# Links of a compressed-attention branch moved in among the query, key and value products, and conv taps and gate products moved within the attention

## The chip, the cores and the metric

One core of a Trainium2 chip runs the whole program. The time is that of the device, in microseconds (us), from the start to the end of one execution; lower is better. Three executions of the kernel before gave 759.12, 759.73 and 758.73 us, median 759.12 us.

The engines are named as in the profile: PE (TensorE, the matrix engine; PEld is its loading of the stationary operand), DVE (VectorE), ACT (ScalarE), POOL (GpSimd) and SP (SyncE, which issues the DMAs here). SBUF is the on-chip memory, PSUM the eight banks of 512 f32 per partition into which PE writes.

## The reference, cut to what matters

One layer with 512 positions, 1024 features and 8 heads in 2 groups. Left out here are the norms, the conv branch's last steps and the whole MLP behind it, which the change does not touch.

```
proj = rms_norm(x) @ w_in      # q | k_c v_c k_s v_s k_w v_w | g_nsa | u_conv | g_merge
# compressed branch: overlapping blocks of 32 positions, stride 16, become one key and one value each
def compress(kv, pe, w1, w2):
    blk = kv[:, idx] + pe                       # 31 blocks x (32*64) per group
    return gelu(blk @ w1) @ w2
kc, vc = compress(k_c, pe_k, ck1, ck2), compress(v_c, pe_v, cv1, cv2)
p_c = softmax(q . kc * scale - slope * dist)    # masked; the "cmp scores"
o_c = p_c @ vc
o_s, o_w = attention over the selected blocks and over the window (k_s, v_s and k_w, v_w)
o = sigmoid(g)[0] * o_c + sigmoid(g)[1] * o_s + sigmoid(g)[2] * o_w
# conv branch
z = a * sigmoid(gate); z = causal_dwconv(z, width 31); y_conv = silu(layer_norm(z)) @ w_conv_br
x = x + (sigmoid(g_a) * (o @ w_attn_br) + sigmoid(g_b) * y_conv) @ w_out
x = x + conv_ffn(rms_norm(x)); out = rms_norm(x)
```

With 8 blocks of 64 positions and a top-16 choice, all blocks are selected, and the window is as long as the sequence, so that the kernel does two dense causal attentions for each head beside the compressed one.

## The kernel before, in words

**Precision.** Every f32 operand of a large product is split into a high part and a low part (a cast on ACT, a subtraction on DVE or POOL), and a product is three PE products: high x high, high x low, low x high. `gemm` (L275) yields after every PE product, so that a caller can take one at a time; with K=8 it is 24 products of 512 columns.

**Weights.** The class `Weights` (L33) brings units of 1 MB by SP's queue (two `raw` buffers), and each unit's two halves are split into `wh` (ACT, L91) and `wl` (POOL, L93), four buffers of each.

**Order.** The code is traced in a program order, and a scheduler then orders each engine's queue: it takes, at each point of its own modelled time, the earliest instruction in program order that it holds to be ready. Each engine then runs its queue in that order and waits where an input is not there. Program order is therefore a priority, not the order itself.

**PSUM.** `psum(tag, name)` (L267) takes a bank of a tag: `mm`, `s` and `t` have two banks each, `o` and `y` one each. `psum_any` (L270) goes round `mm`, `s`, `t`. A bank is free again when the last reader of its former tile has finished.

**SBUF.** `big` (L132) takes one of 27 slots of 4 KB per partition.

**The stage of the change (L485 to L583).** First come the conv branch's input (four chunks `zy`), then `ck`, `cv` (the compressed branch's keys and values, L523), the four query products q0 to q3 (L530), the two key products k0, k1 (L547) and the value products (L566: 96 products of 280 columns into four banks, of which the loop over `kq` does a quarter each time). The compressed branch is a chain of links for k and one for v: `blocks` (DVE, ACT), `hidden` (16 PE products, then ACT L392 and DVE L393), `gelu` (two PE products `hTk`/`hTv` at L398, then ACT L400), then for k `comp_k` (ACT L408, DVE L409, two PE products `kc` at L412 and L413, then ACT and DVE), and for v `comp_v` (ACT, DVE, four PE products `vc` at L430, then ACT L433, DVE L434 and others). In the kernel before, `hidden("k")` stands behind q1, `hidden("v")` behind q3, `gelu("k")` behind k0, `gelu("v")` behind k1, and `comp_k` and `comp_v` after both, ahead of the value products. `cmp_scores` (L440) does 16 PE products of 64 columns (`sc`) for one half of the positions, then a softmax on DVE, POOL and ACT.

**The conv taps.** Each of the four chunks has one ACT instruction (`first`, L493) and 30 DVE instructions (`tap`, L499), 31 items, all appended to the list `pend`. `bg(n)` (L294) traces the next n of them. `bg(BG0)` traces 80 ahead of the cmp scores; the remaining 44 are traced in the attention, each behind the latest row reduction (`last["ttr"]`, DVE L707), and none earlier on DVE than that. From `conv_sum` on (steps `CONV_AT`) the conv branch's LayerNorm follows, up to `cB` (L671, L672).

**The attention (L784 to L812).** 16 steps (8 heads x 2 kinds), cut into 133 pieces (`atoms`): `qk` (PE products `s` at L721 and L727, DVE L707, ACT exp L709), `soft` (DVE L735, then POOL or DVE L739), `ptr` (PE transposes `t` L749, ACT L752, DVE L753) and `pv` (PE products `o` L763 and L769, ACT L775, DVE L777). Between the pieces `fill(n)` traces n of 480 filler products: the 16 merge-gate products (`g`, 384 PE products, bank tag `mm`, each evicted by ACT L593), then the 96 products `cb` of the conv branch, which need `cB`. Before the `cb` products stand four sigmoids on ACT (L601), placed behind the latest exp.

The number of fillers after a piece is this line, and that of taps the one above it:

```
        bg(-(-len(pend) // max(1, nbg - n)))
        fill(int(left[0] / (len(atoms) - n + 0) * 1.1 + 0.5))
```

Behind the attention come the branch projections (`ab`, L837), the merge, the output projection `o0acc` and the MLP (`ua`, `uv`, `d0acc`), which the change leaves as they are.

Of the kernel before, what the change touches and what calls it, by code (L numbers as in the profile page):

```python
# [115 lines left out]
def hybrid_block_kernel(ctx: ExitStack, tc: tile.TileContext, x, norm1_g, w_in, cmp_pe_k, cmp_pe_v,  # L116
# [150 lines left out]
    def psum(tag, name, pl=None):  # L267
        return psB.tile([P, S], F32, tag=tag, name=name, bufs=NB[tag])

    def psum_any(name):  # L270
        tag = ("mm", "s", "t")[cyc[0] % 3]
        cyc[0] += 1
        return psum(tag, name)
# [20 lines left out]
    def bg(n):  # L294
        for _ in range(min(n, len(pend))):
            pend.pop(0)()
# [88 lines left out]
    def hidden(kv):  # L385
        ws = W.get(f"w1{kv}", 0, lead=1) + W.get(f"w1{kv}", 1)
        ps = psum_any(f"hid{kv}")
        for j in range(16):
            mm(ps[:, :256], lhsT=BL[kv][j // 8][:, j % 8].rearrange("p a b -> p (a b)"),
               rhs=ws[j // 4][:, j % 4].rearrange("p a b -> p (a b)"), start=(j == 0), stop=(j == 15))  # L390
        t1 = big(f"ht{kv}", (P, 2, P))
        act.copy(t1[:, 0], ps[:, P : 2 * P])  # L392
        vec.tensor_tensor(t1[:, 1], ps[:, 0:P], t1[:, 0], op=ALU.add)  # L393
        HT[kv] = t1

    def gelu(kv):
        p2 = psum_any(f"hT{kv}")
        mm(p2[:, :64], lhsT=HT[kv][:, 1], rhs=J, start=True, stop=True)  # L398
        ge = cf[:, 4 + "kv".index(kv)]
        act.activation(ge, p2[:, :64], AF.Gelu_apprx_tanh)  # L400
        GEL[kv] = ge

    kc = bp.tile([P, 2, 2, 32], F32R, tag="kc", name="kc")
    vc = bp.tile([P, 2, 2, 64], F32R, tag="vc", name="vc")

    def comp_k():
        gl = cr[:, 6:8]
        act.copy(gl[:, 0], GEL["k"])  # L408
        vec.tensor_tensor(gl[:, 1], GEL["k"], gl[:, 0].bitcast(F32), op=ALU.subtract)  # L409
        ps = psum_any("kc")  # L410
        rhs = gl.rearrange("p a b -> p (a b)")
        mm(ps[:, :P], lhsT=w2kH, rhs=rhs, start=True, stop=False)  # L412
        mm(ps[:, :P], lhsT=w2kL, rhs=rhs, start=False, stop=True)  # L413
        t1, t2 = cf[:, 6], cf[:, 7]
        act.copy(t1, ps[:, 64:128])
        vec.tensor_tensor(t2, ps[:, 0:64], t1, op=ALU.add)
        t2v = t2.rearrange("p (g n) -> p g n", g=2)
        act.copy(kc[:, :, 0], t2v)
        vec.tensor_tensor(kc[:, :, 1], t2v, kc[:, :, 0].bitcast(F32), op=ALU.subtract)

    def comp_v():
        gr = big("gr", (P, 2, 2, 4, 32), F32R)
        src = GEL["v"].rearrange("p (g n) -> p g n", g=2).unsqueeze(2).broadcast_to([P, 2, 4, 32])
        act.copy(gr[:, 0], src)
        vec.tensor_tensor(gr[:, 1], src, gr[:, 0].bitcast(F32), op=ALU.subtract)
        for g in range(2):
            ps = psum_any(f"vc{g}")
            rhs = w2vHL.rearrange("p a b -> p (a b)")
            for part in range(2):
                mm(ps[:, :P], lhsT=gr[:, part, g].rearrange("p a b -> p (a b)"), rhs=rhs,  # L430
                   start=(part == 0), stop=(part == 1))
            t1, t2 = cf[:, 8 + 2 * g], cf[:, 9 + 2 * g]
            act.copy(t1, ps[:, 64:128])  # L433
            vec.tensor_tensor(t2, ps[:, 0:64], t1, op=ALU.add)  # L434
            act.copy(vc[:, g, 0], t2)
            vec.tensor_tensor(vc[:, g, 1], t2, vc[:, g, 0].bitcast(F32), op=ALU.subtract)
# [3 lines left out]
    def cmp_scores(ib):  # L440
        pc = big(f"pc{ib}", (P, 2, 8, 32))
        st = bp.tile([P, 3, 16], F32, tag="cst", name=f"cst{ib}", bufs=2)
        pcf = pc.rearrange("p i h n -> p (i h) n")
        for ii in range(2):
            i = 2 * ib + ii
            ps = psum_any(f"sc{i}")
            pv = ps.rearrange("p (h a n) -> p h a n", h=8, a=2)
            for h in range(NH):
                mm(pv[:, h].rearrange("p a n -> p (a n)"), lhsT=QS[h // 2][:, h % 2, i * P : (i + 1) * P],
                   rhs=kc[:, h // 4].rearrange("p a n -> p (a n)"), start=True, stop=True)  # L450
            vec.tensor_tensor(pc[:, ii], pv[:, :, 1], ndc[:, i].unsqueeze(1).broadcast_to([P, 8, 32]), op=ALU.add)
            vec.tensor_tensor(pc[:, ii], pv[:, :, 0], pc[:, ii], op=ALU.add)
        vec.tensor_reduce(st[:, 0], pcf, axis=AX.X, op=ALU.max)
        vec.tensor_tensor(pcf, pcf, st[:, 0].unsqueeze(2).broadcast_to([P, 16, 32]), op=ALU.subtract)
        pool.tensor_tensor(pc, pc, sl.unsqueeze(1).unsqueeze(3).broadcast_to([P, 2, 8, 32]), op=ALU.mult)
        act.activation(pc, pc, AF.Exp)
        vec.tensor_reduce(st[:, 1], pcf, axis=AX.X, op=ALU.add)
        vec.reciprocal(st[:, 2], st[:, 1])
        gv = gate[:, 2 * ib : 2 * ib + 2].rearrange("p i (h b) -> p i h b", b=3)[:, :, :, 0]
        s2 = st[:, 2].rearrange("p (i h) -> p i h", i=2)  # L460
        vec.tensor_tensor(s2, s2, gv, op=ALU.mult)
        pool.tensor_tensor(pcf, pcf, st[:, 2].unsqueeze(2).broadcast_to([P, 16, 32]), op=ALU.mult)
        PC.append(pc)
# [59 lines left out]
    for i, kv in enumerate("kv"):  # L523
        ps = psum_any(f"c{kv}")
# [5 lines left out]
    for u in range(2):  # L530
        for i in range(2):
            c = 2 * u + i
            ps = psum_any(f"q{c}")
            run(gemm(ps, W.get(f"q{u}", i), h1))
            qs = big(f"qs{c}", dt=F32R)
            for e in range(2):
                a, b = slice(64 * e, 64 * e + 64), slice(64 - 64 * e, 128 - 64 * e)
                act.activation(qs[a, e], ps[a], AF.Copy, scale=QSC[2 * c + e])
                vec.scalar_tensor_tensor(qs[b, e], ps[a], QSC[2 * c + e], qs[a, e].bitcast(F32),
                                         op0=ALU.mult, op1=ALU.subtract)  # L540
            QS.append(qs)
            if c == 1:
                hidden("k")
            elif c == 3:
                hidden("v")
    KK = {}
    for b in range(2):  # L547
        ps = psum_any(f"k{b}")
        run(gemm(ps, W.get("k", b), h1))
        kf = big(f"kf{b}")[:, 0]  # L550
        act.copy(kf, ps)
        for g in range(2):
            kk = big(f"kk{b}{g}", dt=F32R)
            a, o_ = slice(64 * g, 64 * g + 64), slice(64 - 64 * g, 128 - 64 * g)
            for d in (a, o_):
                act.copy(kk[d, 0], kf[a])
            vec.tensor_tensor(kk[a, 1], kf[a], kk[a, 0].bitcast(F32), op=ALU.subtract)
            pool.tensor_tensor(kk[o_, 1], kf[a], kk[a, 0].bitcast(F32), op=ALU.subtract)
            KK[b, g] = kk
        gelu("kv"[b])  # L560
    comp_k()
    comp_v()
    VV = bp.tile([P, 4, 4, 2, 64], F32R, tag="vv", name="VV")
    gate = cp.tile([P, 4, 24], F32, name="gate")
    vps = [psum_any(f"v{t}") for t in range(4)]
    for kq in range(4):  # L566
        wv = W.get(f"v{kq // 2}", kq % 2)
        for t in range(4):
            for hp, wpart in ((0, 0), (1, 0), (0, 1)):
                for k in range(2):  # L570
                    mm(vps[t][:, :280], lhsT=h1[2 * kq + k][:, hp, t * P : (t + 1) * P], rhs=wv[wpart][:, k, :],  # L571
                       start=(kq == 0 and k == 0 and hp == 0 and wpart == 0), stop=(kq == 3 and wpart == 1 and k == 1))
    for t in range(4):
        ps = vps[t]
        vsrc = ps[:, :256].rearrange("p (a d) -> p a d", d=64)
        act.copy(VV[:, :, t, 0], vsrc)
        vec.tensor_tensor(VV[:, :, t, 1], vsrc, VV[:, :, t, 0].bitcast(F32), op=ALU.subtract)
        act.copy(gate[:, t], ps[:, 256:280])
# [34 lines left out]
    def fill(n):  # L613
        for _ in range(n):
            if left[0] == 0:
                return
            next(fg, None)
            left[0] -= 1
        if left[0] == 0:
            run(fg)  # L620


    cv, last = {}, {}
    BG0 = 80
    CONV_AT = (6, 8, 9, 10)

    def csum(nm):
        t = big(nm)[:, 0]
# [153 lines left out]
                OT.append(ot)  # L782

    bg(BG0)  # L784
    cmp_scores(0)
    fill(12)
    cmp_scores(1)
# [17 lines left out]
    for n, f in enumerate(atoms):  # L805
        f()
        if pend and n >= 3:
            with tc.issue_after(last["ttr"].ins):
                bg(-(-len(pend) // max(1, nbg - n)))
        fill(int(left[0] / (len(atoms) - n + 0) * 1.1 + 0.5))  # L810
    pv(15)
    fill(left[0])  # L812
    assert next(fg, None) is None and len(sig) == 16
# [198 lines left out]
```

## Time and profile before

| what | us |
|---|---|
| median of three executions | 759.12 |
| the profiled execution | 759.77 |
| its span (first to last instruction of the program) | 758.1 |
| PE busy in the span | 735.7 |
| DVE busy | 446.3 |
| ACT busy | 345.8 |
| POOL busy | 195.6 |

The span is the profile's time axis, with 0 at the first instruction; the profiled execution's 759.77 us is 1.67 us more, for what lies around the span. "Busy" is the time in which an engine runs an instruction; "idle before" is time in which its next instruction waits. In the rows further down "x16" is a count, "<-DVE cr" names what released a waiting instruction, and PEclk is the granted share of TensorE's clock: 1.00 is 2.4 GHz, 0.50 is 1.2 GHz. The trace's record of a PE product lasts from its start to the end of its pipeline, longer than the distance to the next one; the row of the chain, where pieces do not overlap, gives the distance.

### The profile page before, as it was taken

To read this page: it belongs to the slowest core of one execution; us is meant where nothing else is said; L and a number is where in the kernel's file an instruction comes from. 1 tells how busy PE (TensorE), PEld (TensorE's weight loads), DVE (VectorE), ACT (ScalarE), POOL (GpSimd) and SP (SyncE) were. 2 spreads that over 40 slices of the span, in tenths; PEclk is the share of its full clock that TensorE was granted. 3 is DMA by queue.
4 is the path that set the end of the run, shared out by engine and by line. 5 is a ranking of instruction groups with operands and counts; after the bars stand their busy time and mean duration, and the time that the engine had idled before them with its cause. 6 is when DMAs were issued, how large, how long until landed. Compare 5 with 4: busy or idle time off the path is not lost.

```text
span 758.1 us, 9262 instructions
## 1 busy us (share of the span) xinstructions
PE 735.7 (97%) x3583; PEld 616.3 (81%) x3583; DVE 446.3 (59%) x774; ACT 345.8 (46%) x591; POOL 195.6 (26%) x144
## 2 busy tenths in 40 slices
PE   7999979999999999989999999999999999999996
PEld 7988869878888867868888888888888888888884
DVE  6479799799757466562176565656565655121225
ACT  5522665555556966642245434443444443212113
POOL 6554665545554632144430000000000000000001
PEclk9999988999999999999999999999999999999998
DMA  7643442311111111115352233233343332232102
GB/s 230 155 130 88 111 127 80 102 57 57 56 55 56 57 55 57 56 59 212 107 207 70 97 112 112 66 101 112 105 175 109 112 109 62 108 112 101 66 1 111
DMA packets 58613, 74.90 MB, mean 99 GB/s; under 512 B 2017, under 2 KB 48457, under 8 KB 58569
## 3 DMA queue, kind: packets, MB, share of 16 engines
q1 hardware_dynamic: 58569, 74.31, 30.4%
q8 instruction: 28, 0.46, 0.3%
q14 instruction: 16, 0.13, 0.1%
HBM read 70.11 MB, written 4.19 MB: 98 GB/s over the span
## 4 chain that ended last, share of the span: by engine, by line
PE 84%; DVE 6%; ACT 3%; issue 2%; DMA 2%; POOL 2%; SPq 1%; POOLq 0%; DVEq 0%; ACTq 0%
PE d0acc L868 15%; PE o0acc L868 6%; PE uv L278 5%; PE uv L284 5%; PE uv L281 5%; PE ua L284 5%; PE ua L281 5%; PE ua L278 5%; PE g L278 4%; PE g L281 4%; PE g L284 4%; PE o L763 2%; PE v L571 2%; DMA raw<-in_w_in_dram 2%; PE t L749 2%
## 5 line engine op out<-in xcount | busy, mean ns | idle before, releaser
L91 ACT CAST wh<-raw 128x1024 fp32r<-128x1024 f32 (+1 forms) x114 | 117.3, 1037 | 207.3 <-PE d0acc L868 69.5
L93 POOL TENSOR_TENSOR wl<-raw,wh 128x1024 fp32r<-128x1024 f32 (+1 forms) x52 | 119.9, 2321 | 147.2 <-ACT wh L91 58.1
L93 DVE TENSOR_TENSOR wl<-raw,wh 128x1024 fp32r<-128x1024 f32 x62 | 75.8, 1223 | 128.9 <-PE d0acc L868 67.9
L978 POOL TENSOR_TENSOR mf<-mf,cst 128x1 f32<-128x1 f32 x4 | 3.7, 929 | 356.3 <-DVE mf L976 356.3
L499 DVE SCALAR_TENSOR_TENSOR cy<-zy,colB,cy 128x482 f32<-128x482 f32 (+28 forms) x116 | 85.3, 736 | 3.9 <-ACT cy L493 1.7
L868 PE MATMUL d0acc<-wh,act 128*128 128x512 f32 x352 | 86.9, 389 | 0.0
L868 PEld LDWEIGHTS d0acc<-wh,act 128*128 128x128 f32 x352 | 66.1, 188 | 13.7
L868 PE MATMUL d0acc<-wl,act 128*128 128x512 f32 x176 | 47.0, 389 | 0.0
L709 ACT ACTIVATE p<-p,st 128x512 f32<-128x512 f32 (+3 forms) x64 | 35.8, 561 | 20.6 <-DVE st L707 20.3
L278 PE MATMUL uv<-h,wh 128*128 128x512 f32 x176 | 44.4, 389 | 0.0
L284 PE MATMUL uv<-h,wl 128*128 128x512 f32 x176 | 43.5, 389 | 0.0
L281 PE MATMUL uv<-h,wh 128*128 128x512 f32 x176 | 43.5, 389 | 0.0
L707 DVE CUSTOM_DVE_ANT_0 p<-s,nd 128x512 f32<-128x512 f32 (+3 forms) x64 | 29.8, 487 | 19.0 <-PE s L721 10.8
L284 PE MATMUL ua<-h,wl 128*128 128x512 f32 x160 | 39.5, 389 | 0.0
L278 PE MATMUL ua<-h,wh 128*128 128x512 f32 x160 | 39.5, 389 | 0.0
L281 PE MATMUL ua<-h,wh 128*128 128x512 f32 x160 | 39.5, 389 | 0.0
L281 PEld LDWEIGHTS uv<-h,wh 128*128 128x128 f32 x176 | 33.0, 188 | 6.9
L868 PEld LDWEIGHTS d0acc<-wl,act 128*128 128x128 f32 x176 | 33.0, 188 | 6.9
L284 PEld LDWEIGHTS uv<-h,wl 128*128 128x128 f32 x176 | 33.0, 188 | 6.9
L278 PEld LDWEIGHTS uv<-h,wh 128*128 128x128 f32 x176 | 32.6, 188 | 6.4
L868 PE MATMUL o0acc<-wh,mg 128*128 128x512 f32 x128 | 35.6, 400 | 1.9 <-DVE mg L847 1.9
L278 PE MATMUL g<-h,wh 128*128 128x512 f32 x128 | 35.8, 412 | 0.1
(382 smaller groups left out, 1442.1 us busy)
## 6 DMA issues: line engine op xcount, KB each, us to landing
raw<-in_ffn_w_up_dram SPq DMA_DIRECT2D x22, 1024.0 KB, 5.1
raw<-in_w_in_dram SPq DMA_DIRECT2D x11, 1024.0 KB, 5.3
raw<-in_ffn_w_down_dram SPq DMA_DIRECT2D x11, 1024.0 KB, 4.9
raw<-in_w_in_dram SPq DMA_DIRECT2D x10, 512.0 KB, 4.0
raw<-in_w_out_dram SPq DMA_DIRECT2D x4, 1024.0 KB, 4.8
x<-in_x_dram SPq DMA_DIRECT2D x4, 512.0 KB, 7.4
raw<-in_w_conv_br_dram SPq DMA_DIRECT2D x2, 1024.0 KB, 5.8
raw<-in_w_attn_br_dram SPq DMA_DIRECT2D x2, 1024.0 KB
```

The lines of the kernel that those rows point to most:

```text
L91: nc.scalar.copy(wh, src)
L93: eng.tensor_tensor(wl, src, wh.bitcast(F32), op=ALU.subtract)
L278: mm(ps, lhsT=wh[:, k, c : c + w], rhs=hs[k][:, 0], start=(k == 0), stop=False)
L281: mm(ps, lhsT=wh[:, k, c : c + w], rhs=hs[k][:, 1], start=False, stop=False)
L284: mm(ps, lhsT=wl[:, k, c : c + w], rhs=hs[k][:, 0], start=False, stop=(k == K - 1))
L499: vec.scalar_tensor_tensor(dst[:, s:], z[:, : S - s], colB[:, 4 * k + c : 4 * k + c + 1], y[:, s:], op0=ALU.mult, op1=ALU.add)
L571: mm(vps[t][:, :280], lhsT=h1[2 * kq + k][:, hp, t * P : (t + 1) * P], rhs=wv[wpart][:, k, :], start=(kq == 0 and k == 0 and hp == 0 and w ...
L707: last["ttr"] = vec.tensor_tensor_reduce(pi, src, nd[:, S - w :], scale=-SLOPE[h], scalar=3e38, op0=ALU.add, op1=ALU.min, accum_out=st[:, ...
L709: last["exp"] = act.activation(pi, pi, AF.Exp, scale=-1.0, bias=st[:, 0, i : i + 1], accum_out=st[:, 1, i : i + 1])
L749: tr(ps[:, o_ : o_ + P], prob(s, i)[:, j * P : (j + 1) * P], ident)
L763: mm(po[:, j * P :], lhsT=VV[:, 2 * b + g, j].rearrange("p a d -> p (a d)"), rhs=PT[s][part][:, KO[j] : KO[j] + S - j * P], start=(b == 0 ...
L868: mm(accs[t][n], lhsT=acts(k)[:, ap, t * P : (t + 1) * P], rhs=w[:, 0, n * S : (n + 1) * S], start=st, stop=sp_)
```

## The change

It moves `gelu("k")` behind q2, `comp_k` behind q3 (ahead of `hidden("v")`), `gelu("v")` behind k0 and `comp_v` into the value products, behind their second quarter. `hT`, `kc` and `vc` take the one bank `o` in place of one of the round; the value products take the `s` and `t` banks, and the cmp scores the `s` banks for the first half of the positions and the `t` banks for the second. 48 items in place of 80 are traced ahead of the attention; the conv branch's four later parts each come a step later, but the first, from 6 to 7. 24 filler products are traced ahead of the first cmp scores, and the factor 1.1 falls away.

```
@@ gelu, comp_k, comp_v, cmp_scores
-        p2 = psum_any(f"hT{kv}")
+        p2 = psum("o", f"hT{kv}")
...
-        ps = psum_any("kc")
+        ps = psum("o", "kc")
...
-            ps = psum_any(f"vc{g}")
+            ps = psum("o", f"vc{g}")
...
-            ps = psum_any(f"sc{i}")
+            ps = psum("st"[ib], f"sc{i}")
@@ the query products
             if c == 1:
                 hidden("k")
+            elif c == 2:
+                gelu("k")
             elif c == 3:
+                comp_k()
                 hidden("v")
@@ the key products
-        gelu("kv"[b])
-    comp_k()
-    comp_v()
+        if b == 0:
+            gelu("v")
@@ the value products
-    vps = [psum_any(f"v{t}") for t in range(4)]
+    vps = [psum("sstt"[t], f"v{t}") for t in range(4)]
...
+        if kq == 1:
+            comp_v()
@@
-    BG0 = 80
-    CONV_AT = (6, 8, 9, 10)
+    BG0 = 48
+    CONV_AT = (7, 9, 10, 11)
@@ ahead of the attention
     bg(BG0)
+    fill(24)
     cmp_scores(0)
@@ between the pieces
-        fill(int(left[0] / (len(atoms) - n + 0) * 1.1 + 0.5))
+        fill(int(left[0] / (len(atoms) - n) + 0.5))
```

## Rows read from the trace of the kernel before

**Rows 1.** The page: busy time of the engines, granted clock in 40 equal slices

```profile
PE 735.7 (97%) x3583; PEld 616.3 (81%) x3583; DVE 446.3 (59%) x774; ACT 345.8 (46%) x591; POOL 195.6 (26%) x144
...
PEclk9999988999999999999999999999999999999998
```

**Rows 2.** PE's waits in the whole span: engine, line, waited for, us, times, longest

```profile
PE kc L412 <- DVE cr L409: 3.8, 1, 3.8
```

**Rows 3.** Two windows: stretch, length, PE PEld DVE ACT POOL, PEclk, DMA share, GB/s

```profile
110.00:112.00 2.00, 1.82 (x8) 1.85 (x9) 1.93 (x4) 1.10 (x3) 0.25 (x1) 0.50 0.41 80
130.00:132.00 2.00, 2.00 (x6) 1.58 (x5) 2.00 (x6) 1.12 (x2) 0.87 (x2) 0.50 0.41 108
```

**Rows 4.** The chain that ended last, 110 to 136: start, us, what

```profile
110.84 7.69 PE v L571 x43
118.53 0.17 PE vc L430 x2
...
120.32 5.49 PE v L571 x42
125.81 3.41 PE sc L449 x31
129.22 3.47 PE g L278 x8
...
134.64 1.82 PE g L284 x8
```

**Rows 5.** PE's timeline: the hT products ahead of the gap (start, us, what)

```profile
106.03 0.33 PE L398 MATMUL hTv<-cf,htv 128*128 128x64 f32 x2
```

**Rows 6.** ACT's timeline around the gap

```profile
103.29 0.22 ACT L400 ACTIVATE cf<-hTk 128x64 f32<-128x64 f32 x1
103.41 2.54 ACT L556 CAST kk<-kf 64x512 fp32r<-64x512 f32 x4
105.97 0.24 ACT L408 CAST cr<-cf 128x64 fp32r<-128x64 f32 x1
107.46 0.41 ACT L688 CAST k<-kk 128x256 fp32r<-128x256 f32 x1 [1.25 <-DVE kk L557]
...
109.15 0.58 ACT L551 COPY kf<-k 128x512 f32<-128x512 f32 x1
```

**Rows 7.** DVE's timeline around the gap

```profile
106.33 1.02 DVE L557 TENSOR_TENSOR kk<-kf,kk 64x512 fp32r<-64x512 f32 x1
107.28 0.73 DVE L499 SCALAR_TENSOR_TENSOR cy<-zy,colB,cy 128x504 f32<-128x504 f32 x1
108.04 0.69 DVE L557 TENSOR_TENSOR kk<-kf,kk 64x512 fp32r<-64x512 f32 x1
...
109.54 0.50 DVE L409 TENSOR_TENSOR cr<-cf,cr 128x64 fp32r<-128x64 f32 x1
```

**Rows 8.** ACT's timeline behind the vc products

```profile
121.02 0.32 ACT L433 COPY cf<-vc 128x64 f32<-128x64 f32 x2
```

**Rows 9.** DVE by line from 128 to 200: the conv taps

```profile
L499 DVE SCALAR_TENSOR_TENSOR cy<-zy,colB,cy 128x490 f32<-128x490 f32 (+28 forms) x50 | 36.8, 737 | 1.1 <-ACT cy L493 0.4
```

**Rows 10.** Windows: the attention's first parts, columns as in rows 3

```profile
128.00:200.00 72.00, 70.67 (x350) 58.43 (x349) 63.54 (x141) 39.98 (x90) 38.03 (x35) 0.98 0.25 78
200.00:264.00 64.00, 64.00 (x335) 53.54 (x334) 36.11 (x86) 44.33 (x93) 35.78 (x32) 1.00 0.18 59
264.00:296.00 32.00, 30.14 (x148) 22.88 (x147) 20.54 (x55) 21.86 (x48) 9.50 (x7) 1.00 0.14 49
```

**Rows 11.** PE's timeline: gate products on both sides of a stretch without them

```profile
153.43 1.78 PE L284 MATMUL g<-h,wl 128*128 128x512 f32 x7
...
162.01 2.06 PE L278 MATMUL g<-h,wh 128*128 128x512 f32 x8
```

**Rows 12.** ACT's timeline: the next gate evictions, and the sigmoids ahead of cb

```profile
160.73 1.07 ACT L593 COPY sig<-g 128x512 f32<-128x512 f32 x2
...
281.70 3.90 ACT L601 ACTIVATE sig<-sig 128x1024 f32<-128x1024 f32 x4
```

## The prediction

> **What bounds the kernel now.** I read the page first. PE is busy 735.7 us, 97% of the span [rows 1], so that only time in which PE waits or works slowly is to be won. The line of the granted clock has one dent, two slices of 19 us each with an 8, from 95 to 133 us [rows 1]: the stage that the change rewrites. PE's waits come next: the longest of the whole span is there, 3.8 us before the first `kc` product, for DVE's low part `cr` (L409) [rows 2]. The windows then show what follows: at 110 to 112 us PE works at 0.50 of its clock, which is 1.2 GHz, and at 130 to 132 again [rows 3]. The chain gives both prices without overlap. 43 value products take 7.69 us (179 ns each) where 42 later ones take 5.49 us (131 ns each), and the first 8 gate products 3.47 us where 8 like them take 1.82 us [rows 4]. The first fall comes behind the gap, the second behind 31 `sc` products of 64 columns, with no gap [rows 3, 4].
>
> Why was `kc` late? `hTv` starts at 106.03 [rows 5], and L409, for which `kc` waits, only at 109.54 [rows 7]. The gelu of k was done at 103.5, but ACT then made four key copies (2.54 us) before the `cr` cast [rows 6], and DVE stood at two key subtractions and at conv taps [rows 7]. Nothing that PE still had was traced between this chain and the value products.
>
> **The change, part by part.** No arithmetic is added or taken away, and 480 fillers stay 480; the sum is over waits, clock and place.
>
> (a) **The gap.** `kc` now stands behind q3, with the 24 products of q3, 24 x 0.227 us (1.82 us for 8 [rows 4]) = 5.4 us, between it and `hTk`; there, no key copies or key subtractions can stand ahead of it. In the row, gelu start to L409's end is 6.75 us [rows 6, 7], and 2.54 us for the copies, 1.25 us for ACT's wait and the two subtractions (1.02 and 0.69 us) are not in the new place. `hTv` is covered by k0 (5.4 us), `vc` by k1 and half of the value products (5.4 + 48 x 0.131 = 11.7 us). I take the whole 3.8 us as gone: -3.8 (0 to -3.8).
>
> (b) **The slow clock behind the gap.** 43 x (179 - 131) ns = -2.1 us (0 to -2.1); it goes with the gap.
>
> (c) **The slow clock behind the scores.** 3.47 - 1.82 = 1.65 us. The change puts 24 fillers ahead of the scores, and the value banks no longer hold the fillers' bank tag, so that 16 scores, 12 fillers, 16 scores can run as traced. Half the short products in a row: I take half, -0.8 (0 to -1.65). The page TensorE: Matmul & The Clock Gate of the Trainium skill (section HAM oscillation) ties the fall to PE standing idle; the row behind the gap agrees, the row behind the scores does not, for there PE stood nowhere idle. By the page alone (c) would be no term of this change and the sum 0.8 us less good; the row decides.
>
> (d) **What is late next in this stage.** The second value bank is now an `s` bank that k1 used, and k1 leaves it with ACT's copy, which ended at 109.73 [rows 6]. Three of the four banks are free before; their first quarter is 18 products, 2.4 us, from 106.4 to 108.8. Left would be 0.9 us. But that copy stood in ACT's queue behind a wait of 1.25 us for a key subtraction, which itself stood behind taps [rows 6, 7], and the 48 items may be done by then. I take +0.5 (0 to 3.3, from 106.4 to 109.73).
>
> (e) **32 items moved into the attention.** 31 of them are taps, 31 x 0.737 = 22.85 us of DVE [rows 9]; one is an ACT instruction, hidden. In program order they come two behind each piece until piece 36, against one from piece 12 on before. DVE is busy 63.5 of 72 us from 128 to 200 and 36.1 of 64 us up to 264 [rows 10]: 8.5 us fit into the first stretch, the other 14.4 us spill into the second, which has 27.9 us free. PE has 1.33 us idle in the first stretch, with 50 taps [rows 9, 10]. I scale it by the taps (1.33 x 81/50 = 2.15): +0.8. The ends are -1.3 (all of that idle goes, since DVE does its work ahead sooner) and +14.4 (the spill holds back every step and PE has nothing to put in).
>
> (f) **Fillers spread to the end.** Ahead of the pieces 48 fillers stand in place of 24; each piece then has 3 at first in place of 4, and the gates' 384th falls behind piece 105 in place of 102. PE's idle from 264 to 296 is 1.86 us [rows 10], the stretch where the gates have run out and the sigmoids (3.90 us on ACT [rows 12]) stand between PE and the `cb` products. The gates last longer, but `cB` is made a step later: I take 0 (-1.9 to +4, twice that idle and a little, since both may miss each other).
>
> SP's and POOL's queues keep their instructions; POOL's splits of the gate weights start when the value products free the buffers, earlier by as much as PE is.
>
> Sum: -3.8 - 2.1 - 0.8 + 0.5 + 0.8 + 0 = **-5.4 us**. Against the profiled execution's 759.77 us (span 758.1 and 1.67 around it) that is 754.4; the profiled one stands 0.65 us above the median, so **753.7** for the median.
>
> **The rivals.**
>
> *One bank for five links.* `vc` of group 1 must wait until `vc` of group 0 has left the bank `o`, and so must `hTv` behind `kc`. For: in the row, `vc` of group 0 was made at 118.70 [rows 4], and ACT took both groups out from 121.02 to 121.34 [rows 8]; with DVE's short sum behind that, of ACT's own length (0.2 us), some 2.9 us. Against: 48 value products (6.3 us) stand behind the first `vc` and need no link. The page Perfetto Trace Analysis (Matmuls) of the Trainium skill says that independent groups should go round the PSUM banks, so that one is evicted while the next is made; here five groups share one, and by that rule the wait is paid. With it, in full: 754.4 + 2.9 - 0.65 = 756.6. Chance 0.10.
>
> *Taps overload DVE.* The place is steps 1 to 8. If a step's reductions queue behind two taps a piece, transposes and `pv` come late, and PE must live on gates. It cannot always: the gate products ended at 155.2 and went on at 162.01 [rows 11], behind two evictions at 160.73 [rows 12], for their two banks were full. It decides once the spill of 14.4 us is not covered by gates; from 5.4 us of uncovered spill on nothing is won, and at the full 14.4 us, on (a) to (d) alone (-6.2), the time is 759.1 - 6.2 + 14.4 = 767.3. Against: DVE takes reductions and taps by turns, and the second stretch has the room. Chance 0.15, at 760.7 to 767.
>
> *Given back.* The gap goes, but the scheduler places the links where they were (already the `sc` products ran 31 in a row with 12 fillers traced between them [rows 4]), or the saved 5 us come back as idle PE where `cb` waits for the later `cB`: 758.5 to 760. Chance 0.11.
>
> *The tail closes too.* Gates that last until the sigmoids take the 1.86 us, and the idle of the first stretch goes as well (-1.3 in place of +0.8): 753.7 - 1.9 - 2.1 = 749.7. Chance 0.16.
>
> **How the numbers follow.** The forecast, 750.5 to 757, has 0.48: **753.7 us**. A measurement of this kernel tells some 0.2%, 1.5 us, from no change, so that faster is below 757.6. Faster: 0.48 + 0.16 + 0.10 = 0.74; within: 0.11; slower: 0.15. The range takes in the tail rival and the lower end of the overload: 748 to 762; it leaves out about 0.04 below and 0.12 above.
>
> **What would show it.** (a), (b): no wait of PE for `cr`, no window under 1.00 between 95 and 125 us, value products at 131 ns throughout. (c): no or a shorter stretch at 0.50 behind the scores. (d), and the one bank: waits of the value products for ACT's `kf` copy, or of `vc` for ACT L433. (e): the last tap later than 198 us by 15 to 25 us, DVE near full until then, and PE's idle in steps 1 to 8 little more than 1.3 us; if it is over 5 us the overload is true. (f): the time between the last gate product and the first sigmoid. I am wrong if PE's gap moves with `kc` to its new place, or if PE waits for transposes in the first half of the attention.

## The result, and the profile after

The kernel after takes **767.32 us** (median of 4 runs, 767.1 to 769.15) against 759.32 for the kernel before on the same chip: ratio **1.0111**, 95% interval 1.0094 to 1.0129 (the ratios given here are not the quotients of two medians). The forecast was 753.7 us with a range of 748 to 762; the sign is wrong. By the profile the span is 765.7 against 758.1 us, 7.6 us longer. Executions of one kernel differ with the mean clock that they were granted (the kernel before, in a later sitting: 755.25 us at 0.996 and 760.92 us at 0.987), so that a slow stretch in one trace need not be in every execution.

To place the 7.6 us I use one tally throughout, called *idle and slow time*: for each PE product, the time from its start to the next one's, less what its form takes in an undisturbed row (227 ns for 128x512, 128 ns for 128x280, 110 ns for the short ones, and so on). Before and after it is 8.3 and 4.6 us from 80 to 140 us, **4.6 and 17.6 us from 140 to 260**, 10.5 and 8.5 from 260 to 350, and 30.9 and 38.5 in all: the same 7.6 us. So the rewritten stage won 3.7 us, the first part of the attention lost 13.0, and what follows it won 2.0.

**The stage of the links.** Of PE's waits after, that of `kc` (columns as in [rows 2]):

```profile
PE kc L412 <- DVE cr L409: 2.3, 1, 2.3
```

Windows of the same kernel (columns as in [rows 3]):

```profile
98.00:100.00 2.00, 2.00 (x7) 1.61 (x7) 1.90 (x4) 0.49 (x2) 1.34 (x1) 0.54 0.94 272
110.00:112.00 2.00, 2.00 (x15) 1.84 (x14) 0.00 (x0) 1.34 (x3) 1.06 (x2) 1.00 0.04 8
130.00:132.00 2.00, 2.00 (x15) 1.82 (x15) 1.71 (x5) 1.25 (x1) 1.84 (x1) 1.00 1.07 373
```

Both stretches of [rows 3] now run at 1.00, but a third at half clock has come, from 98 us on. The gap of [rows 2] has gone *with* `kc` to its new place. ACT's timeline says why:

```profile
90.80 1.05 ACT L91 CAST wh<-raw 128x1024 fp32r<-128x1024 f32 x1 [5.00 <-DMA raw<-in_w_in_dram]
92.59 1.05 ACT L91 CAST wh<-raw 128x1024 fp32r<-128x1024 f32 x1 [0.74 <-DMA raw<-in_w_in_dram]
93.66 0.59 ACT L538 ACTIVATE qs<-q 64x512 fp32r<-64x512 f32 x1
94.27 1.28 ACT L400 ACT_TABLE_LOAD   x1
95.56 0.22 ACT L400 ACTIVATE cf<-hTk 128x64 f32<-128x64 f32 x1
...
96.23 0.24 ACT L408 CAST cr<-cf 128x64 fp32r<-128x64 f32 x1
```

The gelu of k stands behind two casts of the key weights, and the first of them waits 5.00 us for its DMA with ACT idle; a query step (0.59 us) and ACT's table load (1.28 us) follow before the gelu. The kernel before has the same wait at the same place, but there its gelu starts only at 103.29 [rows 6], long after:

```profile
90.71 1.05 ACT L91 CAST wh<-raw 128x1024 fp32r<-128x1024 f32 x1 [5.03 <-DMA raw<-in_w_in_dram]
```

The chain that ended last (start, us, what) then shows the wait, the slow key products and the value products:

```profile
96.51 0.24 DVE cr L409
96.74 0.04 issue
96.79 0.33 PE kc L412
97.12 0.11 PE kc L413
97.22 1.00 PE hidv L389 x8
98.23 3.38 PE k L278 x8
101.61 1.86 PE k L281 x8
...
111.00 6.21 PE v L573 x48
...
123.86 1.84 PE g L278 x8
...
129.33 1.71 PE sc L449 x16
131.03 1.92 PE g L278 x8
132.96 0.91 PE g L281 x4
133.86 1.15 PE sc L449 x11
```

8 key products take 3.38 us where the next 8 take 1.86. The value products begin no earlier than before (110.84 in [rows 4]), then run at 129 ns each, with no wait for `vc` or for a bank; behind the scores the clock stays up.

**The attention.** Windows of the kernel after (the stretches of [rows 10], and two more):

```profile
101.00:146.00 45.00, 45.00 (x260) 40.09 (x259) 23.03 (x46) 28.18 (x55) 28.43 (x18) 0.99 0.37 115
128.00:200.00 72.00, 69.42 (x359) 56.94 (x358) 56.40 (x134) 41.20 (x93) 38.04 (x37) 1.00 0.24 74
200.00:264.00 64.00, 58.57 (x286) 46.19 (x285) 55.55 (x126) 36.77 (x88) 24.74 (x25) 0.97 0.10 34
230.00:252.00 22.00, 16.68 (x87) 11.74 (x85) 21.21 (x55) 14.46 (x41) 9.66 (x13) 0.99 0.16 49
264.00:296.00 32.00, 29.83 (x153) 24.28 (x152) 15.04 (x35) 26.41 (x44) 13.87 (x8) 1.00 0.22 67
```

The first of these stretches in the kernel before:

```profile
101.00:146.00 45.00, 41.18 (x228) 37.19 (x227) 40.88 (x74) 27.53 (x56) 26.22 (x17) 0.89 0.29 92
```

DVE is busy 23.0 of the 45 us from 101 to 146 (before: 40.9). From 128 to 200 it does *less* than before, 56.4 in place of 63.5 us; from 200 to 264 it has 55.6 in place of 36.1, and there PE loses 5.4 us where it lost none. From 230 to 252 DVE is full (21.2 us) and PE works 16.7 of 22 us. The waits of PE that the profile names from 200 to 264 add up to 5.2 us: 3.5 for DVE, and 1.7 for a softmax step on POOL, which itself stood idle for 9.05 us until DVE's reciprocal (L739) came. The line of the taps (L499) shows where they went; in the kernel before there are 31 from 101 to 146:

```profile
L499 DVE SCALAR_TENSOR_TENSOR cy<-zy,colB,cy x2: 724/730/735, 101.1 to 145.8; 128x497 f32<-128x497 f32 x1, 128x498 f32<-128x498 f32 x1
L499 DVE SCALAR_TENSOR_TENSOR cy<-zy,colB,cy x71: 702/739/754, 145.8 to 247.4; 128x498 f32<-128x498 f32 x3, 128x499 f32<-128x499 f32 x3, 128x500 f32<-128x500 f32 x3, 128x501 f32<-128x501 f32 x3
L499 DVE SCALAR_TENSOR_TENSOR zy<-zy,colB,cy x3: 717/737/749, 163.0 to 248.2; 128x511 f32<-128x511 f32 x3
```

The 46 taps ahead are done by 102 us, and the next follows at 145.8, behind the row reductions to which the rest are tied; the last starts at 248.2. In the kernel before it starts at 198.5:

```profile
L499 DVE SCALAR_TENSOR_TENSOR zy<-zy,colB,cy x4: 733/746/747, 79.4 to 198.5; 128x511 f32<-128x511 f32 x4
```

And PE's timeline has no gates to put in while it waits:

```profile
228.83 1.75 PE L284 MATMUL g<-h,wl 128*128 128x512 f32 x7
230.65 0.40 PE L284 MATMUL g<-h,wl 128*128 128x512 f32 x1
251.28 1.64 PE L644 MATMUL cmean<-csum,ones 128*128 128x512 f32 x2 [0.40 <-DVE csum L635]
251.93 2.69 PE L278 MATMUL g<-h,wh 128*128 128x512 f32 x4
```

After 288 gate products PE has none for 21 us, until the conv mean is through: the mean's tile is traced before the 289th product and takes a bank of the gates' two.

### The profile page after: what moved, and what is told of

Same layout as the page of the kernel before. It is cut to its first block, busy times and chain, and to the rows that moved or that the text cites. A ratio compares the mean times of both kernels' runs of the same rounds, so it can differ in the third digit from the quotient of the medians.

```text
span 765.7 us, 9271 instructions
## 1 busy us (share of the span) xinstructions
PE 737.7 (96%) x3583; PEld 615.6 (80%) x3583; DVE 445.0 (58%) x774; ACT 346.7 (45%) x591; POOL 197.5 (26%) x144
## 4 chain that ended last, share of the span: by engine, by line
PE 83%; DVE 7%; ACT 4%; DMA 2%; issue 2%; POOL 1%; SPq 1%; POOLq 0%; DVEq 0%; ACTq 0%
PE d0acc L873 15%; PE o0acc L873 6%; PE uv L278 5%; PE uv L281 5%; PE uv L284 5%; PE ua L278 5%; PE ua L284 5%; PE ua L281 5%; PE g L278 4%; PE g L281 4%; PE g L284 4%; DMA raw<-in_w_in_dram 2%; PE v L573 2%; PE o L767 2%; DVE cy L499 1%
## 5 line engine op out<-in xcount | busy, mean ns | idle before, releaser
L499 DVE SCALAR_TENSOR_TENSOR cy<-zy,colB,cy 128x482 f32<-128x482 f32 (+28 forms) x116 | 85.3, 736 | 3.3 <-ACT cy L493 1.1
L873 PEld LDWEIGHTS d0acc<-wh,act 128*128 128x128 f32 x352 | 66.1, 188 | 13.7
```

What stands on the lines that cost most here:

```text
L499: vec.scalar_tensor_tensor(dst[:, s:], z[:, : S - s], colB[:, 4 * k + c : 4 * k + c + 1], y[:, s:], op0=ALU.mult, op1=ALU.add)
L873: mm(accs[t][n], lhsT=acts(k)[:, ap, t * P : (t + 1) * P], rhs=w[:, 0, n * S : (n + 1) * S], start=st, stop=sp_)
```

## The experiments

Behind each expectation stand the ratio and, in brackets, its 95% interval, against runs of the kernel before on the same chip. Its median lay between 756.7 and 759.3 us in the sittings, so ratios are compared and not times; ratios whose intervals overlap are not told apart by the time alone. *Ahead* is the number of items traced ahead of the attention; *fillers* means the 24 ahead of the scores and the even spread together.

**First: which part costs?** The stage and the attention part taken apart, and the mean's bank.

The kernel after with 80 items ahead:

```
-    BG0 = 48
+    BG0 = 80
```

> The changed kernel with 80 items traced ahead of the attention again in place of 48; all else as changed. Theory A (the 32 items moved into the attention cost it all): the last tap comes near 200 us in place of 248, the stretch from 232 to 251 us without gate products goes, and with it the 10 us or so that PE loses there; the time is then below that of the kernel before by what the links and the scores win, 3 to 5 us: 754 to 756.5. Theory B (the later conv steps and the even spread of the fillers cost it): the last tap is early, but the time stays at 764 to 768.

1.0058 (1.0037 to 1.0079). Half of the loss goes: not all, as Theory A had it, and a little more than Theory B allowed. The links now wait: `vc` 1.9 us for DVE's `gr`, as DVE has its taps again. The 24 fillers and the later conv steps are still in this run.

The kernel before with 48 ahead:

```
-    BG0 = 80
+    BG0 = 48
```

> The kernel before with the one number changed, 48 items ahead in place of 80. Theory A: taps last to 235 us or later, the conv branch's mean comes after them, and the time rises by 8 to 15 us: 767 to 774. Theory B: within 2 us of the kernel before.

**0.9976** (0.9956 to 0.9995): faster, by little, and within 2 us of the kernel before, as Theory B had it. So fewer items ahead are not the cause by themselves. Without any link moved the wait of `kc` falls from 3.8 to 1.6 us and the clock doesn't fall from 80 to 215 us (idle and slow time 2.2 us from 80 to 140, 8.3 before). The last tap comes at 231.7, and from 140 to 260 PE loses 10.4 us, 5.8 more than before, which takes back nearly all of the 6.1 that the stage won. What is left of the gain lies behind: from 260 to 350 idle and slow time is some 6 us, against 10.5 before.

The links alone:

```
 (the kernel after, with)
-    BG0 = 48
-    CONV_AT = (7, 9, 10, 11)
+    BG0 = 80
+    CONV_AT = (6, 8, 9, 10)
-    fill(24)
-        fill(int(left[0] / (len(atoms) - n) + 0.5))
+        fill(int(left[0] / (len(atoms) - n + 0) * 1.1 + 0.5))
```

> The kernel before with the links moved and the banks changed, and nothing else of the change: 80 items ahead, conv steps 6, 8, 9, 10, the factor 1.1, no 24 fillers ahead of the scores. By the trace of the changed kernel the gap before kc is 2.3 us in place of 3.8 and one slow stretch of 3.4 us in place of one of 6.8; the slow stretch behind the scores may come back without the 24 fillers. Both theories: 755 to 758.5, 1 to 4 us below the kernel before. If the links themselves cost the attention time (theory C), 760 or more.

1.0013 (0.9995 to 1.0031): moved links win nothing, against the expectation of 1 to 4 us. PE's waits in the stage:

```profile
PE vc L430 <- DVE gr L425: 2.5, 1, 2.5
PE kc L412 <- DVE cr L409: 2.5, 1, 2.5
```

One gap of 3.8 us has become two of 2.5, each with a slow stretch behind it.

The conv statistics in a bank of their own:

```
-        ps = psum("mm", "cmean")
+        ps = psum("y", "cmean")
 (the same for "cvar" and "crs")
```

> The changed kernel with the three tiles of the conv branch's LayerNorm (mean, variance, 1/deviation) in the taps' bank y, which is free once the last tap is read, in place of the tag mm that the gate products use. 48 items ahead as changed. It tells how theory A's loss comes about. A1 (the gate products stop because the mean's tile stands before them in the round of mm banks and waits for the last tap): gate products go on between 232 and 251 us and the time falls by 6 to 10 us, to 757 to 761, though the taps still end near 245. A2 (DVE is simply too late for the attention's own steps): the time stays within 3 us of 767.

1.0102 (1.0077 to 1.0127). The time is that of A2, though the sign of A1 came: behind the 288th gate product PE now has none for 6.7 us in place of 21, and it is busy 62.4 of 64 us from 200 to 264. But from 264 to 296:

```profile
264.00:296.00 32.00, 23.94 (x121) 19.05 (x120) 17.71 (x45) 27.73 (x49) 11.04 (x8) 0.89 0.10 33
```

The gates have run out at 269.7, the first `cb` product comes at 287.5, behind `cB`, whose last cast on ACT starts at 283.2 (in the kernel before: 261.6), and 8.1 us are lost here in place of 2.2. In this kernel the bank only says *where* the loss falls.

**Second: the attention part, piece by piece.**

The kernel before with the conv steps and fillers of the kernel after, 80 ahead:

```
-    CONV_AT = (6, 8, 9, 10)
+    CONV_AT = (7, 9, 10, 11)
     bg(BG0)
+    fill(24)
...
-        fill(int(left[0] / (len(atoms) - n + 0) * 1.1 + 0.5))
+        fill(int(left[0] / (len(atoms) - n) + 0.5))
```

> The kernel before with the conv steps a step later (7, 9, 10, 11), 24 more fillers ahead of the scores and an even spread of the rest; links and the 80 items ahead as before. Theory S (the later, evenly spread part costs by itself): the difference between the two earlier runs that differ in it, 1.0058 against 1.0013, comes again: ratio 1.004 to 1.006, last tap after 205 us, conv mean after 235 us, PE's idle and slow time from 140 to 260 us 8 us or more (4.6 before). Rival L (it costs only together with the moved links): ratio 0.998 to 1.001.

1.0041 (1.0027 to 1.0056); idle and slow time from 140 to 260 is 9.0 us. So the conv steps and fillers cost by themselves, with the taps early.

The kernel after with conv steps and fillers as before (links and 48 alone), that is, the run of the links alone with 48 in place of 80:

```
-    BG0 = 80
+    BG0 = 48
```

> The changed kernel with conv steps, 24 fillers and spread as before: the moved links and the 48 items ahead alone. If the parts simply add (48 alone gave 0.9976, links alone 1.0013): ratio 0.997 to 1.000, last tap near 232 us. If the links and the 48 items collide (the links' DVE and ACT work behind fewer taps is early, so that the loss must then be elsewhere): over 1.004.

0.9990 (0.9975 to 1.0004): the two parts add. The wait of `kc` is 2.3 us, that of `vc` gone.

The kernel after with only the conv steps back:

```
-    CONV_AT = (7, 9, 10, 11)
+    CONV_AT = (6, 8, 9, 10)
```

> The changed kernel with only the conv steps put back to 6, 8, 9, 10. Theory C (the later steps spread the taps thinner, two a piece instead of three, so that conv mean, cB and the cb products come late and the gates run out): last tap near 232 to 236 us in place of 248, conv mean by 240, ratio 1.000 to 1.004. Theory F (the 24 fillers ahead and the even spread use up PE's gates early): last tap earlier all the same, but ratio still 1.007 to 1.011.

**1.0196** (1.0171 to 1.0222), against both theories: the last tap comes at 250.6, and the loss nearly doubles. The mean is traced earlier, and the gates stop already at 264 products, as PE's timeline shows:

```profile
224.52 0.62 PE L284 MATMUL g<-h,wl 128*128 128x512 f32 x2
254.18 1.14 PE L644 MATMUL cmean<-csum,ones 128*128 128x512 f32 x2
```

PE has no gates from 225 to 258, the clock falls for 10 us, and 24.3 us are lost from 140 to 260. Beside late taps and the fillers the later conv steps of the change are thus a help; without the fillers they are not, as the next run (1.0018) beside the one above (0.9990) suggests.

The kernel after with only the fillers back:

```
-    fill(24)
...
-        fill(int(left[0] / (len(atoms) - n) + 0.5))
+        fill(int(left[0] / (len(atoms) - n + 0) * 1.1 + 0.5))
```

> The changed kernel with only the 24 fillers ahead taken out and the factor 1.1 back; conv steps stay at 7, 9, 10, 11. Theory C: last tap stays near 248 us and the ratio at 1.007 to 1.011. Theory F: ratio 1.000 to 1.004, and the first stretch of over 5 us without fillers, now at 164 us, comes after 200 us or not at all.

1.0018 (1.0001 to 1.0036), as Theory F had it, though the last tap came earlier too, at 237.8. From 140 to 260 PE loses some 9.3 us in place of 17.6.

The kernel after without the 24 ahead, but evenly spread:

```
     bg(BG0)
-    fill(24)
     cmp_scores(0)
```

> The changed kernel without the 24 fillers ahead of the scores, but with the even spread (factor 1.0) and its late conv steps. Theory P (the 24 ahead bring the gates to their two full banks in step 3, where ACT's copies stand behind the attention's): no stretch of over 8 us without fillers from 150 to 200 us, last tap by 240 us, ratio 1.000 to 1.004, as with both undone (1.0018). Theory E (the even spread does it): ratio 1.007 to 1.011.

1.0011 (0.9987 to 1.0035): of the fillers it is the 24 ahead that cost. With them 5.4 us of gates stand ahead of the attention, whose first step then starts at 138 in place of 133 us and whose fourth at 166 in place of 157, and the taps, tied to pieces, come later with them. Yet 17.1 us without gates remain, from 226.5, so that such a stretch alone does not make the loss.

**Third: the queues.** Is it the fillers, or the taps that wait for the pieces? And does the gap come from ACT's queue?

64 ahead, on the run with links and 48 alone:

```
-    BG0 = 48
+    BG0 = 64
```

> The moved links with 64 items ahead, conv steps and fillers as before. If the DVE's free time from 101 to 146 us (some 20 us) is what the 48 leave unused: last tap 215 to 222 us in place of 235, the 17.6 us without fillers at 221 us shrinks to under 8, ratio 0.993 to 0.997, and vc still finds its gr made in time. If the links need the DVE as free as with 48: a wait of vc for gr of over 1 us with a slow clock behind it, ratio 0.999 to 1.002.

0.9993 (0.9970 to 1.0017): the second expectation. `vc` waits 2.5 us for `gr` behind the extra taps; what the attention wins (4.3 us of idle and slow time, from 9.9) the stage loses (10.6, from 4.6).

The gelu of k and the `cr` cast ahead of the key weights' casts, on the same run (0.9990):

```
+    def gelu_k():
+        gelu("k")
+        gl = cr[:, 6:8]
+        c1 = act.copy(gl[:, 0], GEL["k"])
+        with tc.issue_after(c1.ins):
+            W.get("q1", 1)
...
-            run(gemm(ps, W.get(f"q{u}", i), h1))
+            run(gemm(ps, W.get(f"q{u}", i, lead=1 if c == 2 else 2), h1))
...
-                gelu("k")
+                gelu_k()
```

> The moved links with 48 items ahead (the run that gave 0.9990), and in ACT's queue the gelu of k and the cr cast stand ahead of the two casts of the key weights. Theory Q (the gap moved with kc because the gelu waited in ACT's queue behind those casts, which waited 5 us for their DMA): PE's 2.3 us wait for cr falls to under 0.4 us, the stretch of slow clock from 98 us goes, PE's idle and slow time from 80 to 140 us falls from 4.6 to under 2 us; the time falls by 2 to 4 us, ratio 0.993 to 0.997, if the attention doesn't give it back. Rival W (the chain hidk, hTk, gelu, cr is too long by itself): the wait stays over 1.5 us. Rival G (given back): the wait goes, the ratio stays at 0.998 to 1.000.

**0.9962** (0.9945 to 0.9980). ACT's timeline (lines behind the new function are 6 higher):

```profile
88.18 1.28 ACT L400 ACT_TABLE_LOAD   x1
89.47 0.23 ACT L400 ACTIVATE cf<-hTk 128x64 f32<-128x64 f32 x1
89.73 0.25 ACT L409 CAST cr<-cf 128x64 fp32r<-128x64 f32 x1
90.62 1.05 ACT L91 CAST wh<-raw 128x1024 fp32r<-128x1024 f32 x1 [0.65 <-DMA raw<-in_w_in_dram]
```

Of PE's waits in the same run, that of `kc`:

```profile
PE kc L418 <- DVE cr L415: 0.5, 1, 0.5
```

The gelu starts at 89.47 in place of 96.16, in time in which ACT had stood idle; the wait falls from 2.3 to 0.5 us, and the slow stretch at 98 us is gone. So the wait had the cause that Theory Q names. (A slow stretch from 125.8 us on, at the scores, takes 1.7 us of it back.) The intervals of 0.9990 and 0.9962 just overlap; the last run below repeats the step.

Both together (the gelu ahead, and `BG0 = 64`):

> Both: the gelu ahead of the key weights' casts and 64 items ahead. If each takes its part: ratio 0.988 to 0.994, no slow clock from 85 to 215 us. If what is won ahead of the attention is given back in it: not under 0.996.

0.9978 (0.9959 to 0.9996), no gain over the gelu alone. The number is that of the second expectation, but not its reason: idle and slow time falls in the attention (from 140 to 260) to some 4 us, and the loss lies ahead of it, where `vc` waits 3.6 us for `gr`, as with the 64 above.

16 of the items that the pieces would bring (15 taps and one ACT instruction), in DVE's queue behind `gr`:

```
     bg(BG0)
+    with tc.issue_after(GEL["gr"]):
+        bg(16)
 (GEL["gr"] is the instruction that makes gr's low part)
```

> The run with the gelu ahead and 48 items (0.9962), and 16 taps of those left stand in DVE's queue behind gr, the last thing that a link wants of DVE, in place of behind the row reductions of the attention. Theory T (with 48 items DVE stands idle from 101 to 146 us and the taps end too late): no wait of vc, last tap 218 to 224 us in place of 232, the 17.4 us without fillers at 218 us under 8 us, ratio 0.990 to 0.994. Rival O (the taps' place doesn't matter, what is won comes back where the gates run out): last tap earlier, ratio 0.995 to 0.998.

0.9950 (0.9931 to 0.9970): no wait of `vc`, the last tap at 217.2, but the ratio is at the edge of rival O and not told apart from 0.9962: stretches of 7.1 and 8.4 us without fillers come later, at 240.5 and 272.

The same with `bg(32)` (31 taps and one ACT instruction):

> The same with 32 taps behind gr. Theory T: last tap 203 to 212 us, ratio 0.988 to 0.993, unless the scores' softmax on DVE is held back by the taps (then DVE waits show from 125 to 150 us, and no more is won than with 16). Rival O: 0.995 to 0.998.

**0.9909** (0.9880 to 0.9938), 752.09 us against 758.6: as Theory T had it, and the best of the study. The last tap comes at 203.1, and no window of the attention up to 264 is short of PE work by more than 1.3 us (windows, columns as in [rows 3]):

```profile
101.00:146.00 45.00, 45.00 (x256) 39.93 (x255) 37.48 (x75) 28.41 (x58) 30.27 (x18) 0.96 0.36 116
146.00:200.00 54.00, 52.72 (x271) 43.01 (x270) 48.78 (x104) 30.02 (x69) 27.34 (x29) 1.00 0.19 59
200.00:264.00 64.00, 63.73 (x336) 53.08 (x335) 37.88 (x99) 45.66 (x100) 35.74 (x34) 1.00 0.15 50
```

The deciding one, **the kernel after itself with 32 taps behind `gr`**, fillers and conv steps untouched:

```
 (the kernel after, with)
     bg(BG0)
+    with tc.issue_after(GEL["gr"]):
+        bg(32)
```

> The changed kernel as it is, with 32 of its moved taps in DVE's queue behind gr. Theory T: last tap 208 to 216 us in place of 248, the 21.3 us without fillers at 231 us under 9 us, ratio 1.002 to 1.006 in place of 1.0111 (as with 80 items ahead, 1.0058, but without its wait of vc). Theory P alone (the 24 fillers ahead and the full banks, whatever the taps do): ratio over 1.008.

**0.9992** (0.9973 to 1.0012): lower than Theory T's own range. Its windows:

```profile
101.00:146.00 45.00, 45.00 (x262) 40.09 (x261) 34.91 (x65) 28.04 (x54) 27.44 (x17) 1.00 0.35 114
146.00:200.00 54.00, 50.64 (x261) 40.91 (x260) 47.56 (x114) 32.52 (x79) 28.53 (x30) 1.00 0.18 59
200.00:264.00 64.00, 63.87 (x334) 52.82 (x333) 43.06 (x105) 38.01 (x88) 29.98 (x29) 1.00 0.15 50
```

DVE does 34.9 in place of 23.0 us from 101 to 146 with PE full all the same; the last tap comes at 209.9, and PE's 5.4 us from 200 to 264 are back. What remains is 3.4 us of idle PE from 146 to 200, where the best run, with fillers and conv steps as before, has 1.3. The 13.7 us without gates from 163.7 are still there, and so is the gap of `kc` (2.2 us).

The kernel after with the gelu ahead (the diff above, on the kernel after):

> The changed kernel as it is, with the gelu of k and the cr cast ahead of the key weights' casts in ACT's queue. Theory Q: the wait of kc falls from 2.3 to about 0.5 us and the slow clock at 98 us goes, the time falls by 2 to 4 us, ratio 1.006 to 1.009. Given back in the attention: 1.010 to 1.012.

1.0076 (1.0049 to 1.0103): some 0.35% of the loss was the gap that moved, and the attention doesn't give it back. The list of PE's waits from 85 to 130 us is empty. This pair's intervals too overlap a little, but the same step took 0.3% off both kernels.

## Why the prediction was wrong

**(a) and (b), the gap and the slow clock behind it, -5.9 us: wrong by two thirds.** The step that failed is "I take the whole 3.8 us as gone". I checked which of the old neighbours could not stand in the new place (key copies, key subtractions) and not which neighbours are new there. ACT does its queue in order in these rows, and in the new place two casts stand ahead of the gelu that wait for a transfer. The trace of the kernel before already showed that wait (5.03 us, at 90.71). 2.3 us of wait and some 1.5 us of slow clock (3.38 against 1.86) came back, and with them out of the way the time fell (0.9990 to 0.9962, 1.0111 to 1.0076). The sign that would make me wrong, "if PE's gap moves with `kc` to its new place", is what came. The page TensorE: Matmul & The Clock Gate of the Trainium skill (section HAM oscillation) has the clock fall after PE stood idle; the row behind the gap of 2.3 us shows such a fall, though the rule there is for longer gaps, and with 80 ahead (the run at 1.0058) a gap of 2.5 us before `kc` has no slow stretch behind it until 119 us. So not every gap of this length brings one.

**(c), the scores, -0.8 us: right in the trace, its reason not shown.** The clock stays up behind the scores, and the whole 1.65 us came. In all six traces in which 12 gates split the scores into 16 and 16 it stays up. But of the nine traces with 31 or 32 scores in a row it falls at them in only four, so that one trace of each kernel doesn't show that the split did it. The 24 ahead don't bring the split by themselves: in the kernel before with them (1.0041) the 32 still ran in a row.

**(d) and the rival of one bank.** The rival was rightly held unlikely, and (d) took 0.5 us too much. The value products wait for no bank and `vc` waits for nothing; the +0.5 was not needed.

**(e), 32 items moved, +0.8 us: the step that decided.** I forecast the last tap 15 to 25 us later; it is 50 us later. The failed sentence is "8.5 us fit into the first stretch, the other 14.4 us spill into the second". I counted DVE's room as if the moved taps would fill it from 128 us on. They are tied to the pieces and start only at 145.8; 22 us of DVE's time from 101 to 146 stay empty, and the first stretch, far from filling up, holds 7 us less DVE work than before. From 200 to 264 DVE has 19.4 us more (55.6 against 36.1), not 14.4, and there PE waits for it. What was +0.8 us came as 13.0 us from 140 to 260, the fillers' part in it. I scaled PE's idle by the number of taps (1.33 x 81/50), as if the loss were in proportion; it begins when DVE is full and the fillers are gone.

**The overload rival was the right mechanism**, priced at 760.7 to 767 and at 767.3 for a full spill, where 767.32 was measured; the exact agreement is luck, for the price used all of (a) and (b) and no cost of the fillers. I gave it 0.15 on "the second stretch has the room". It had 27.9 us free and has 8.4 left, and PE waits there all the same: room in a stretch's sum is not room in each step's turn.

**(f), fillers, 0 us: wrong.** The failed sentence is "I take 0": I looked at the far end only, where the idle went from 1.86 to 2.17 us. The cost starts at the near end: 24 gates ahead put the steps, and the taps with them, later, and the gates reach their two full banks at 164.5 us, and ACT's copies that empty them come at 176.3, behind work of the attention. Without the 24 the ratio is 1.0011; PE is then busy 52.6 in place of 51.4 us from 146 to 200 and 60.9 in place of 58.6 from 200 to 264, so that the larger part falls where the taps are late. The stretch at the full banks is not the loss by itself, for it stands in the run at 0.9992 too.

**How the parts combine.** Neither the 24 fillers (1.0111 without them 1.0011) nor the tied taps (0.9992 when 32 of them are untied) cost the kernel 1% alone: either undone, the loss goes. Where the taps are early, fillers and conv steps together cost some 0.4% (1.0041); where the fillers are as before, the late taps cost nothing (0.9990 beside 1.0013). Both put the last tap later: it comes at 248.2, without the 24 at 239.9, with 32 untied at 209.9. And 48 ahead on the kernel before *win* a little (0.9976): the stage wins what the late taps cost, and the stretch from 260 to 350 is better by some 4 us, for a reason that wasn't looked into.

What stays open: how much of the later conv steps' help in the kernel after is due to the bank order of the mean, and how much to the taps' slower drain; the two weren't varied apart. Open too is why fillers and late taps cost more together than each alone; that the fillers are then gone while DVE is full is read from the traces, not varied.

## What to carry to other kernels

When a step is moved earlier, read each engine's queue at the *new* place: a copy that waits for a transfer there (here 5.00 us) holds back what stands behind it in the queue, however ready that is. When work is taken out of one stage, ask what else can use the engine's time there: work tied to later steps can't, and the hole can be paid for when that engine becomes full. Here queueing 32 items right behind the last instruction that the links need kept the links free and the engine busy, and it was worth some 0.5% (0.9962 to 0.9909), where moving the links alone won nothing (1.0013).

## What the runs showed that was not expected

With the conv steps a step earlier the time rose another 0.8% over the kernel after (1.0196), where less was expected: the mean, which shares the gates' banks, was traced earlier, and the gates stood for 33 us. That the bank did it is not shown, for the pace of the taps changed with it.

The clock can also fall with PE busy throughout. In the run with the gelu ahead the chain has 32 short scores in a row, no wait of PE over 0.5 us from 85 to 130, and a slow stretch from 125.8 to 129.2. The chain that ended last:

```profile
121.98 0.91 PE g L281 x4
122.89 3.94 PE sc L455 x32
126.83 1.87 PE g L281 x4
```

A window of the same run:

```profile
126.00:129.00 3.00, 3.00 (x10) 2.52 (x11) 2.92 (x6) 0.23 (x1) 1.05 (x1) 0.50 0.93 314
```

Here, as in [rows 3, 4], the clock fell with no idle time of PE ahead of it, which the section of the Trainium skill named above (TensorE: Matmul & The Clock Gate, HAM oscillation) does not speak of. But in the run with links and 48 alone the same 32 scores (3.49 us) brought no fall, so a row of short products is not enough to tell.
